# Prompt attention in a hybrid decoder layer: query, key and bias rows laid out by head, and a third half-step scored inside the projection

## The chip, the core and the metric

The kernel runs on one core of a Trainium2 chip. A core has a matrix engine (PE, whose weight loads are listed apart as PEld), a vector engine (DVE), an activation engine (ACT), a general engine (POOL) and a queue engine (SP) that here only issues transfers; each works through its own list of instructions in order, and they wait for each other by semaphores. Transfers (DMA) move data between DRAM, the on-chip memory (SBUF) and back; matrix products end in PSUM banks. The metric is the device time of one execution in microseconds (us), the median over several runs.

## The reference

One layer of a decoder is computed for a prompt of 2048 tokens and for a group of 8 samples of 4 tokens, both in float32. The projection `z = h @ w_in` is cut into the inputs of four branches; the prompt's stick-breaking attention is the branch that the change touches:

```python
h = rms_norm(x, pre_g)
z = h @ w_in
ca, cb, cg, pu, pg, q, k, v, sg, mq, mg = jnp.split(z, ...)   # conv, pool, attention, memory

def sb_block(q, k, v, bias, q_pos, k_pos):
    z = einsum('nqhd,nkhd->nhqk', q, k) * (SB_HEAD_DIM ** -0.5) + bias[None, :, None, None]
    mask = (k_pos[None, :] < q_pos[:, None])[None, None]
    log_beta = log_sigmoid(z)
    log_1m = where(mask, log_sigmoid(-z), 0.0)
    rc = cumsum(log_1m, axis=3, reverse=True)
    a = exp(where(mask, log_beta + rc - log_1m, -inf))
    return einsum('nhqk,nkhd->nqhd', a, v)
```

There are 8 heads of 64 and one bias per head. So the weight of a key is beta = sigmoid(z) times the product of (1 - beta) over all keys between it and the query: a running product along the keys, from the query backwards. The outputs of all branches are multiplied by gates, joined, multiplied by `w_out`, normalised and added to the input.

## The kernel before, in words

The work runs in three long stages. After a short start the **projection** goes through the columns of `w_in` in groups, for the first 1056 columns of tokens (half 0) and then the other 1024 (half 1); each product is three passes over high and low parts of the operands (line 251). `z_evac` takes each finished tile out of PSUM. Beside it run side generators (`tasks`): the depthwise convolution on DVE (`conv_dw`, line 642, 12 tile steps of `cacc` at the end of the last channel), the memory attention and the sample group's paged attention. The **prompt attention** then goes over 4 pairs of heads (`hp`) and 4 blocks of 512 queries (`qb`), and for each over the key blocks `kc` from the diagonal downwards. A piece of 2 times 128 queries of one head is a half-step, named `hp_qb_kc_hh_q2` (hh: head of the pair; q2: 0 or 2, its first block of 128 queries). The **out-projection** comes last.

For one half-step `sb_scores` multiplies queries with keys into a PSUM tile `S` (two products of 128 and of 66 rows: high parts, low parts, and two rows that add the bias), `sb_gates` makes beta in `be` and 1 - beta in `gam` on ACT, DVE runs the product along the keys (`tensor_tensor_scan`, tile `E`; its second operand `ZM` is a PSUM tile copied by ACT from `zm`, which POOL fills), POOL multiplies `be` by `E`, PE transposes the result (`turn`, line 1398), ACT copies it out, and PE multiplies it with the values (line 1410). Where `rest_of` holds, 1 - beta is made on DVE (line 1358) instead of ACT.

Queries and keys reach this stage through DRAM: `z_evac` (line 721) writes a tile's high and low part with one transfer into `qd` or `kd`, whose layout has the two heads of a pair as 128 partitions; `bias_rows` writes the bias and rows of ones into `bd` (line 467); `load` (lines 1260 to 1281) reads 16 transfers per (hp, qb): for each head the key's high part twice, the query's high and low part, the key's low part, the query's high part again, and the two bias rows of each.

The first two half-steps, 0_0_0_0_0 and 0_0_0_1_0, are scored early: `sb_early` runs as a side generator at the end of the projection, starts once the sample group is done, and keeps 1 - beta and beta of both in the tile `early`.

The order of every engine but PE is set when the program is built, by a scheduler that simulates the program; PE runs in the order in which the code is written. Transfers are issued in order on SP's list, too. The convolution's second part (`conv_post`, lines 1460 to 1500) loads `cy` from DRAM (line 1471) and adds four channel groups on POOL into `cs` (line 1478); its first load and sum are side work with no place in the written order of POOL and SP.

Of the kernel before, what the change touches and what calls it, by code (L numbers as in the profile page):

```python
# [8 lines left out]
F32 = mybir.dt.float32  # L9
# [3 lines left out]
AF = mybir.ActivationFunctionType  # L13
# [5 lines left out]
P = 128  # L19
D = 1024  # L20
ND = D // P
SEQ = 2048
# [70 lines left out]
def kernel(  # L93
# [29 lines left out]
    dram = ctx.enter_context(tc.tile_pool(name="dram", bufs=1, space=DRAM))  # L123
    qd = dram.tile([4, P, 2, SEQ], F32, name="qd")
    kd = dram.tile([4, P, 2, SEQ], F32, name="kd")
    vd = dram.tile([SEQ, 512], F32, name="vd")
# [17 lines left out]
    mvd = dram.tile([4, P, 2, 2 * P], F32, name="mvd")  # L144
    bd = dram.tile([NH + 1, 2, 512], F32, name="bd")
    c11d = dram.tile([8, P, 512], F32, name="c11d")
# [307 lines left out]
    def bias_rows():  # L454

        b = zc.tile([NH, 1], F32, name="brow")
        sp.dma_start(b, sb_bias.rearrange("o h -> h o"))
        hl = zc.tile([NH, 2], F32R, name="bhl")
        t = k4("brows", [P, 2, 512], F32)
        pool.memset(t[: NH + 1], 1.0)  # L460
        for _ in range(3):
            yield
        dve.tensor_copy(hl[:, 0:1], b)
        dve.tensor_tensor(out=hl[:, 1:2], in0=b, in1=hl[:, 0:1].bitcast(F32), op=ALU.subtract)
        for x in range(2):
            dve.tensor_copy(t[:NH, x], hl[:, x : x + 1].bitcast(F32).to_broadcast([NH, 512]))
        sp.dma_start(bd, t[: NH + 1])

# [237 lines left out]
    def z_evac(part, kind, c, ti, c0, c1, ps, s):  # L706
# [5 lines left out]
        if kind in ("q", "k"):  # L712
            zt = small(f"zt{nm}")
            before = table[6] if nm == "0q0_0" else casts[-1] if state["mem"] else None
            with tc.issue_after(before.ins) if before is not None else ExitStack():
# [4 lines left out]
                               op=ALU.subtract)  # L720
            wq.dma_start((qd if kind == "q" else kd)[c, :, :, tok : tok + np_], hl[:, :, :np_].bitcast(F32))
            if N > np_:
# [533 lines left out]
    def sb_loader(sbr):  # L1256
# [3 lines left out]
        def load(hp, qb):  # L1260
            tok = slice(512 * qb, 512 * qb + 512)
            Q = []
            for hh in range(2):
                pr = slice(64 * hh, 64 * hh + 64)
                slot = qb if qb or hp % 2 == 0 else 4
                kts = [(sbr if slot < 2 else KT["pool"]).tile([P, 512], F32R, tag=f"k{n}{slot}", name=f"k{n}{hp}_{qb}_{hh}",
                                                              bufs=2) for n in "hl"]
                qt_ = sbr.tile([P, 2, 512], F32R, tag="Q", name=f"Q{hp}_{qb}_{hh}", bufs=4)
                for x in range(2):
                    hx = slice(64 * x, 64 * x + 64)  # L1270
                    sp.dma_start(kts[0][hx].bitcast(F32), kd[hp, pr, 0, tok])
                    sp.dma_start(qt_[hx, 0].bitcast(F32), qd[hp, pr, x, tok])
                sp.dma_start(kts[1][:64].bitcast(F32), kd[hp, pr, 1, tok])
                sp.dma_start(qt_[:64, 1].bitcast(F32), qd[hp, pr, 0, tok])
                sp.dma_start(kts[1][64:66].bitcast(F32), bd[2 * hp + hh])
                sp.dma_start(qt_[64:66, 1].bitcast(F32), bd[NH])
# [12 lines left out]
    def sb_scores(S, q2, w, Q, kts):  # L1289
        for j in range(2):  # L1290
            c = slice(P * (q2 + j), P * (q2 + j + 1))
            pe.matmul(S[:, j, :w], lhsT=Q[:, 0, c], rhs=kts[0][:, :w], start=True, stop=False)  # L1292
            pe.matmul(S[:, j, :w], lhsT=Q[:66, 1, c], rhs=kts[1][:66, :w], start=False, stop=True)  # L1293

# [5 lines left out]
    def sb_early(load, values, blk, sbr, bps, early):  # L1300

        room = sbr.tile([P, 16, P], F32, tag="V", name="early", bufs=2).rearrange("p (n j b) c -> p n j (b c)", n=4, j=2)
        for n in range(2):
            blk[0, n] = load(0, n)
        values(0)
        for _ in range(4):
            yield
        for hh in range(2):
            S = bps.tile([P, 512], F32, tag="AT", name=f"Se{hh}", bufs=2).rearrange("p (j k) -> p j k", j=2)
            Q, KT, _ = blk[0, 0]  # L1310
            sb_scores(S, 0, 2 * P, Q[hh], KT[0, hh, 0])
            early[hh] = room[:, 2 * hh], room[:, 2 * hh + 1]
            sb_gates(S, 2 * P, *early[hh])
            yield

    def sb_prompt(load, loaded, sb, bps, ops, zmp, early, values_of, flags, newest):
# [18 lines left out]
        def score(hp, qb, kc, hh, q2, Q, KT, carry):  # L1335
# [4 lines left out]
            w = ns[1]  # L1340
            rest_of = q2 == 2 and (dg or hh == 0)
            if (hp, qb, q2) == (0, 0, 0):
                ga, be = early[hh]
            else:
                S = ops.tile([P, 2, 512], F32, tag="S", name=f"S{nm}", bufs=2)
                sb_scores(S, q2, w, Q[hh], KT[hp, hh, kc])
                be = sb.tile([P, 2, 512], F32, tag="be", name=f"be{nm}", bufs=BEB)
                g_ = gam[count["pair"] % 3]
                count["pair"] += 1
                ga = g_[:, :, 512 - w : 512]  # L1350
                sb_gates(S, w, None if rest_of else ga, be[:, :, :w])
# [853 lines left out]
```

## Time and profile before

| | us |
|---|---|
| median of the runs (3 runs) | 2327.63 |
| lowest and highest run | 2325.99, 2337.69 |
| the profiled execution's own time | 2329.11 |
| its span in the profile | 2327.4 |
| projection, about | 30 to 1474 of the span |
| prompt attention, about | 1474 to 1880 |
| out-projection, to the end | 1880 to 2327 |
| busy PE / DVE / ACT / POOL | 2252.0 / 1716.6 / 1079.3 / 1317.9 |

A row of a timeline gives the start in us from the start of the span, the busy time in us, the engine, the line, the operation and its tiles (written<-read, buffer numbers left out), the shape and a count; in brackets stands the idle time of that engine just before and what ended it. SPq rows are transfers being issued. A row of a view by stretches of time gives the stretch and its length, then the busy us and (in brackets) the instructions of PE, PEld, DVE, ACT and POOL, the granted share of PE's clock, the mean busy share of the DMA engines and GB/s. A row of waits tells which instruction waited for which: us in total, times, longest.

### The profile page before, as it was taken

What the parts mean: (1) busy time and instruction counts of PE and PEld (TensorE: products, weight loads), DVE (VectorE), ACT (ScalarE), POOL (GpSimd) and SP (SyncE); (2) the same over time, 40 slices, a digit from 0 to 9 for tenths busy, and PEclk for the clock granted to TensorE, in tenths of its full rate; (3) what the DMA queues carried; (4) which work ended last, traced back from release to release, by engine and by line L of the source; (5) the groups of instructions that cost most, each with busy time, mean ns of one, the idle gap of its engine ahead of it and who ended that gap; (6) DMA issues with size and microseconds to landing.
All of it is one profiled execution on the core that took longest, in us unless ns stands there. A gap on an engine that the chain in (4) does not pass through costs nothing. (4 is left out here: it accounts for less than half of the span.)

```text
span 2327.4 us, 43469 instructions
## 1 busy us (share of the span) xinstructions
PE 2252.0 (97%) x16512; PEld 1815.3 (78%) x16512; DVE 1716.6 (74%) x2303; ACT 1079.3 (46%) x1975; POOL 1317.9 (57%) x1410
## 2 busy tenths in 40 slices
PE   7999999999999999999999999999999999999997
PEld 7998888888888777777777777667766668787775
DVE  5343786969647764477786867899999876686997
ACT  5332343342442322224242334588888876453553
POOL 3554546556474655545546455489999964432332
PEclk9999999999999999999999999899999999999999
DMA  6689977878679899987977884666545207876774
GB/s 213 200 284 323 337 265 261 285 249 286 245 254 307 308 355 335 336 287 270 319 253 233 298 275 149 166 199 200 158 132 133 76 20 233 290 231 190 248 248 145
DMA packets 338189, 558.32 MB, mean 240 GB/s; under 512 B 29163, under 2 KB 213611, under 8 KB 321581
## 3 DMA queue, kind: packets, MB, share of 16 engines
q1 hardware_dynamic: 282604, 286.83, 39.8%
q0 software_dynamic: 55376, 268.72, 32.4%
q8 instruction: 130, 2.13, 0.4%
q14 instruction: 79, 0.64, 0.1%
HBM read 465.35 MB, written 90.72 MB: 239 GB/s over the span
## 5 line engine op out<-in xcount | busy, mean ns | idle before, releaser
L990 DVE STREAM_TRANSPOSE T<-kt 128x1024 f32<-128x1024 f32 x256 | 308.6, 1226 | 182.2 <-PE sSA L1003 174.7
L957 POOL DMA_INDIRECT vt<-in_cache_v_dram,idv x256 | 253.1, 989 | 257.0 <-PE sO L1042 195.9
L642 DVE SCALAR_TENSOR_TENSOR cacc<-U,par,cacc 128x512 f32<-128x512 f32 x480 | 359.8, 750 | 11.0
L1379 POOL TENSOR_TENSOR be<-be,E 128x512 f32<-128x512 f32 (+4 forms) x316 | 314.1, 1004 | 25.4 <-DVE E L1370 13.0
L957 POOL DMA_INDIRECT kt<-in_cache_k_dram,idk x128 | 128.7, 1006 | 196.1 <-DVE T L990 155.2
L1370 DVE TENSOR_TENSOR_SCAN E<-gam,cr,ZM 128x513 f32<-128x513 f32 x192 | 230.7, 1261 | 4.7 <-POOL csq L1490 1.0
L2024 PE MATMUL acc<-wohi,mh 128*128 128x512 f32 (+1 forms) x480 | 192.0, 400 | 0.2 <-ACT mh L1748 0.2
L2024 PE MATMUL acc<-wolo,mh 128*128 128x512 f32 (+1 forms) x480 | 188.4, 392 | 0.7 <-DVE wolo L1659 0.7
L2024 PE MATMUL acc<-wohi,ml 128*128 128x512 f32 x448 | 177.2, 395 | 6.5 <-DVE ml L1759 6.5
L1400 ACT COPY at<-AT 128x512 f32<-128x512 f32 (+1 forms) x288 | 154.6, 598 | 44.2 <-PE AT L1398 39.0
L1398 PE MATMUL AT<-ident,be 128*128 128x128 f32 x1082 | 155.9, 283 | 17.4 <-ACT at L1400 11.7
L1398 PEld LDWEIGHTS AT<-ident,be 128*128 128x128 f32 x1082 | 122.1, 144 | 59.6 <-issue 23.8
L1298 ACT ACTIVATE be<-S 128x1024 f32<-128x1024 f32 (+1 forms) x158 | 154.2, 976 | 9.9 <-PE S L1293 7.5
L1003 PE MATMUL sSA<-T,W 128*32 128x128 f32 x4096 | 138.2, 276 | 1.8 <-DVE T L990 1.4
L1410 PE MATMUL av<-at,V 128*64 128x256 f32 (+1 forms) x1152 | 137.0, 378 | 0.5 <-DVE sgt L1414 0.3
L1292 PE MATMUL S<-kh,Q 128*128 128x512 f32 (+1 forms) x316 | 134.6, 430 | 1.5 <-ACT be L1298 1.5
L1003 PEld LDWEIGHTS sSA<-T,W 128*32 128x32 f32 x4096 | 104.5, 109 | 36.7 <-issue 29.1
L1759 DVE TENSOR_TENSOR ml<-mr,mh 128x512 fp32r<-128x512 f32 x108 | 92.3, 862 | 40.4 <-ACT mh L1748 39.6
L1410 PEld LDWEIGHTS av<-at,V 128*64 128x64 f32 x1152 | 76.4, 138 | 58.4 <-issue 23.5
L1042 PE MATMUL sO<-vt,saT 128*32 128x512 f32 x1024 | 122.0, 592 | 0.0
L1293 PE MATMUL S<-kl,Q 66*128 66x512 f32 (+1 forms) x316 | 120.7, 386 | 0.0
L1748 ACT CAST mh<-mr 128x512 fp32r<-128x512 f32 (+1 forms) x120 | 70.3, 594 | 89.9 <-PE acc L2024 26.0
(591 smaller groups left out, 6254.5 us busy)
## 6 DMA issues: line engine op xcount, KB each, us to landing
mr<-mixd SPq DMA_DIRECT2D x32, 512.0 KB
Q<-qd SPq DMA_DIRECT2D x96, 128.0 KB
mr<-mixd SPq DMA_DIRECT2D x48, 256.0 KB
xtp<-in_x_prompt_dram SPq DMA_DIRECT2D x16, 512.0 KB
kh<-kd SPq DMA_DIRECT2D x64, 128.0 KB
ws<-in_w_out_dram SPq DMA_DIRECT2D x16, 512.0 KB
wsd<-ws SPq DMA_DIRECT2D x16, 512.0 KB
msd<-mr SPq DMA_DIRECT2D x32, 256.0 KB
```

The lines of the kernel that those rows point to most:

```text
L642: dve.scalar_tensor_tensor(out=ps, in0=U[:, a + k : a + k + H], scalar=wd[:, k : k + 1], in1=ps, op0=ALU.mult, op1=ALU.add)
L957: pool.indirect_dma_start(out=dst, out_offset=None, in_=rows, in_offset=bass.IndirectOffsetOnAxis(ap=idx, axis=0))
L990: S["turn"] = dve.transpose(T[:, 2 * hh : 2 * hh + 2].rearrange("p s j t -> p (s j t)"), kt[:, 2 * hh : 2 * hh + 2].rearrange("p s j d -> ...
L1003: pe.matmul(sSs[n][32 * g : 32 * g + 32, P * ml : P * (ml + 1)], lhsT=W[:, jj, :], rhs=T[:, :, jj, :], start=i == 0, stop=i == 3, tile_pos ...
L1292: pe.matmul(S[:, j, :w], lhsT=Q[:, 0, c], rhs=kts[0][:, :w], start=True, stop=False)
L1298: act.activation(out=be, in_=S[:, :, :w], func=AF.Sigmoid)
L1370: dve.tensor_tensor_scan(out=E[:, j][:, ::-1], data0=g_[:, j][:, ::-1], data1=ZM[:, 0:1].to_broadcast([P, 513]), initial=carry[hh, q2][:, ...
L1379: newest.append(pool.tensor_tensor(out=be[:, j, :m], in0=be[:, j, :m], in1=E[:, j, 513 - w : 513 - w + m], op=ALU.mult).ins)
L1398: pe.transpose(ap_[:, n : n + P], A[hp, qb, kc, hh, qt][:, P * r : P * (r + 1)], ident)
L1400: act.copy(at[:, :n], ap_[:, :n])
L1410: pe.matmul(av[64 * hh : 64 * hh + 64, c], lhsT=V[:, 4 * kc + r, 64 * hh : 64 * hh + 64], rhs=ats.pop((hp, qb, kc, hh, q2, r)), start=dg a ...
L2024: pe.matmul(o[:rows], lhsT=m[a][:, k, :rows], rhs=W[prod, 4 * h + k][w], start=not cont and h == k == n == 0, stop=h == 1 and k == 3 and n ...
```

## The change

1. **Layout.** `qd` and `kd` become `[4, 2, 130, 2048]`: each head has 2 rows for bias or ones, 64 rows and 64 rows. For queries these are the high and the low part, for keys the low and the high part. `bd` is gone; `bias_rows` writes the bias rows into `kd` and ones into `qd` with 8 transfers of a block of 512 tokens each instead of one transfer, from two tiles (`brows`, `bones`).
2. **Stores.** `z_evac` writes the high and the low part of a query or key tile with two transfers in place of one; there are 40 such tiles.
3. **Loads.** `load` issues 10 transfers per (hp, qb) in place of 16: the query's two parts come as one transfer of 128 rows, and the low key part and the second query operand come with their bias rows as 66 rows.
4. **Early scores.** `sb_early` waits for two steps of its generator instead of four and scores three half-steps: 0_0_0_0_0, 0_0_0_1_0 and 0_0_0_0_2. The third uses two PSUM tiles, one with the tag of the values' accumulator (`av`) and one with that of the transposes (`AT`). ACT makes only beta of these; 1 - beta is made on DVE in `rest`, since `rest_of` now holds for all three.

```diff
-    qd = dram.tile([4, P, 2, SEQ], F32, name="qd")
-    kd = dram.tile([4, P, 2, SEQ], F32, name="kd")
+    qd = dram.tile([4, 2, P + 2, SEQ], F32, name="qd")
+    kd = dram.tile([4, 2, P + 2, SEQ], F32, name="kd")
...
-    bd = dram.tile([NH + 1, 2, 512], F32, name="bd")
...
-        sp.dma_start(bd, t[: NH + 1])
+        for qb in range(4):
+            for dst, src in ((kd, t), (qd, one)):
+                sp.dma_start(dst.rearrange("a b r t -> (a b) r t")[:, 0:2, 512 * qb : 512 * qb + 512], src[:NH])
+            yield
...
-            wq.dma_start((qd if kind == "q" else kd)[c, :, :, tok : tok + np_], hl[:, :, :np_].bitcast(F32))
+            for x in range(2):
+                r = 2 + DH * (x if kind == "q" else 1 - x)
+                wq.dma_start((qd if kind == "q" else kd)[c, :, r : r + DH, tok : tok + np_], hl[:, x, :np_].bitcast(F32))
...
                 for x in range(2):
-                    hx = slice(64 * x, 64 * x + 64)
-                    sp.dma_start(kts[0][hx].bitcast(F32), kd[hp, pr, 0, tok])
-                    sp.dma_start(qt_[hx, 0].bitcast(F32), qd[hp, pr, x, tok])
-                sp.dma_start(kts[1][:64].bitcast(F32), kd[hp, pr, 1, tok])
-                sp.dma_start(qt_[:64, 1].bitcast(F32), qd[hp, pr, 0, tok])
-                sp.dma_start(kts[1][64:66].bitcast(F32), bd[2 * hp + hh])
-                sp.dma_start(qt_[64:66, 1].bitcast(F32), bd[NH])
+                    sp.dma_start(kts[0][64 * x : 64 * x + 64].bitcast(F32), kd[hp, hh, 66:130, tok])
+                sp.dma_start(qt_[:, 0].bitcast(F32), qd[hp, hh, 2:130, tok])
+                sp.dma_start(kts[1][:66].bitcast(F32), kd[hp, hh, 0:66, tok])
+                sp.dma_start(qt_[:66, 1].bitcast(F32), qd[hp, hh, 0:66, tok])
...
-        for _ in range(4):
-            yield
-        for hh in range(2):
-            S = bps.tile([P, 512], F32, tag="AT", name=f"Se{hh}", bufs=2).rearrange("p (j k) -> p j k", j=2)
-            Q, KT, _ = blk[0, 0]
-            sb_scores(S, 0, 2 * P, Q[hh], KT[0, hh, 0])
-            early[hh] = room[:, 2 * hh], room[:, 2 * hh + 1]
-            sb_gates(S, 2 * P, *early[hh])
+        Q, KT, _ = blk[0, 0]
+        for _ in range(2):
+            yield
+        o = 0
+        for hh, q2, tags in ((0, 0, ("AT",)), (1, 0, ("AT",)), (0, 2, ("av", "AT"))):
+            w = P * (q2 + 2)
+            be = early[hh, q2] = room[:, o : o + 2 * w].rearrange("p (j k) -> p j k", j=2)
+            o += 2 * w
+            S = [bps.tile([P, 512], F32, tag=t, name=f"Se{hh}{q2}{t}", bufs=2 if t == "AT" else 1) for t in tags]
+            if len(S) == 1:
+                S = S[0].rearrange("p (j k) -> p j k", j=2)
+                sb_scores([S[:, j] for j in range(2)], q2, w, Q[hh], KT[0, hh, 0])
+                act.activation(out=be, in_=S, func=AF.Sigmoid)
+            else:
+                sb_scores(S, q2, w, Q[hh], KT[0, hh, 0])
+                for j in range(2):
+                    act.activation(out=be[:, j], in_=S[j], func=AF.Sigmoid)
             yield
...
-            rest_of = q2 == 2 and (dg or hh == 0)
-            if (hp, qb, q2) == (0, 0, 0):
-                ga, be = early[hh]
+            ahead = (hp, qb) == (0, 0) and (hh, q2) in early
+            rest_of = ahead or q2 == 2 and (dg or hh == 0)
+            g_ = gam[count["pair"] % 3]
+            count["pair"] += 1
+            ga = g_[:, :, 512 - w : 512]
+            if ahead:
+                be = early[hh, q2]
```

The scheduler places the work of the other engines anew, and at three places around the end of the projection the lists differ. The last numbers of the names are buffer numbers, and the pair's number in front is left off; `early` is the tile of the early betas, `cs` the convolution's sum over channel groups, `sg1cg_1` and `sg1sg_1` the last two gate tiles of the projection.

On POOL, at the end of the projection, before the change the list reads:

```order
L1106 AFFINE_SELECT nM<-nM 32x32
L1362 MEMSET early 128x2 x2
L1322 MEMSET zm 128x384
L1323 COPY zm<-ident 128x128
L1329 MEMSET gam_14901 128x2
L1329 MEMSET gam_14903 128x2
L1329 MEMSET gam_14905 128x2
L1362 MEMSET be_0_0_0_2_14914 128x2
L1379 TENSOR_TENSOR early<-early,E_0_0_0_0_14916 128x127
```

and with the change:

```order
L1110 AFFINE_SELECT nM<-nM 32x32
L1488 TENSOR_TENSOR cs_19906<-cy_19566 128x256
L1488 TENSOR_TENSOR cs_19906<-cs_19906,cy_19566 128x256 x2
L1331 MEMSET zm 128x384
L1332 COPY zm<-ident 128x128
L1338 MEMSET gam_14942 128x2
L1338 MEMSET gam_14944 128x2
L1338 MEMSET gam_14946 128x2
L1372 MEMSET early 128x2 x3
L1389 TENSOR_TENSOR early<-early,E_0_0_0_0_14950 128x127
```

The three sums into `cs`, which stood some 60 rows further down, behind POOL's products for query block 2, key block 0, head 1 (`be_2_0_1_0`), now stand ahead of `zm`.

On SP, the queue of transfers, the rows around the first load of `cy` read before:

```order
L1271 DMA kh_0_1_15678<-kd 64x512 x2
L1431 DMA sgt_2_15254<-gsd 128x512
L1273 DMA kl_0_1_15679<-kd 64x512
L1275 DMA kl_0_1_15679<-bd 2x512
L1285 DMA V_15689<-vd 128x16x128
L1471 DMA cy_19614<-ydw 128x4x256
```

and with the change:

```order
L1285 DMA V_14783<-vd 128x16x128
L748 DMA gsd<-sg1sg_0_14797 128x512
L651 DMA ydw<-acc_3_1_14919 128x512
L748 DMA gcd<-sg1cg_1_14843 128x512
L566 DMA mixd<-mo_3_512_14856 128x4x128
L1274 DMA Q_2_0_14973<-qd 128x512
L1276 DMA Q_2_0_14973<-qd 66x512
L1095 DMA vsn<-vsd 32x512
L1481 DMA cy_19566<-ydw 128x4x256
L748 DMA gsd<-sg1sg_1_14900 128x512
```

The load of `cy` moved from behind the loads of later blocks to a place among the projection's last stores. With the change it waits for the last product of `z1sg_1`, since its buffer lies where the projection's operands lie.

On ACT, at the end of the projection, before:

```order
L575 CAST pT_3_512_14547<-mpt_3_512_256_14768 128x2x256
L732 ACTIVATE sg1cg_1_14802<-z1cg_1_14775 128x512
L648 COPY acc_3_1_14878<-cacc_3_1_14584 128x512
L732 ACTIVATE sg1sg_1_14852<-z1sg_1_14818 128x512
L1297 ACTIVATE early<-Se_14833 128x512
L1298 ACTIVATE early<-Se_14833 128x512
L1297 ACTIVATE early<-Se_14858 128x512
L1298 ACTIVATE early<-Se_14858 128x512
L1298 ACTIVATE be_0_0_0_2_14914<-S_0_0_0_2_14909 128x1024
L1325 COPY ZM<-zm 128x512
```

and with the change:

```order
L577 CAST pT_3_512_14594<-mpt_3_512_256_14803 128x2x256
L650 COPY acc_3_1_14919<-cacc_3_1_14631 128x512
L1318 ACTIVATE early<-Se00AT 128x512
L736 ACTIVATE sg1cg_1_14843<-z1cg_1_14810 128x512
L1318 ACTIVATE early<-Se10AT 128x512
L1322 ACTIVATE early<-Se02av 128x512
L1322 ACTIVATE early<-Se02AT 128x512
L736 ACTIVATE sg1sg_1_14900<-z1sg_1_14865 128x512
L1298 ACTIVATE be_0_0_1_2_14962<-S_0_0_1_2_14957 128x1024
L1334 COPY ZM<-zm 128x512
```

The copy of the convolution's last accumulator now stands ahead of the gates and the early betas, and on DVE the 12 steps that it waits for stand in one run ahead of the gates; PE has the first early scores after 12 of the 24 products of `z1cg_1`, the second behind the memory attention's product, and the third (`Se02av`, `Se02AT`) after 12 of the 24 products of `z1sg_1`. `Se02av` uses the PSUM bank that this copy frees.

More of the change, by code (lines that the diff above doesn't have):

```diff
@@ L458, in bias_rows @@
         hl = zc.tile([NH, 2], F32R, name="bhl")
-        t = k4("brows", [P, 2, 512], F32)
-        pool.memset(t[: NH + 1], 1.0)
+        t, one = k4("brows", [P, 2, 512], F32), k4("bones", [P, 2, 512], F32)
+        pool.memset(one[:NH], 1.0)
         for _ in range(3):
@@ L1263, in load @@
             for hh in range(2):
-                pr = slice(64 * hh, 64 * hh + 64)
                 slot = qb if qb or hp % 2 == 0 else 4
@@ L1291, in sb_scores @@
             c = slice(P * (q2 + j), P * (q2 + j + 1))
-            pe.matmul(S[:, j, :w], lhsT=Q[:, 0, c], rhs=kts[0][:, :w], start=True, stop=False)
-            pe.matmul(S[:, j, :w], lhsT=Q[:66, 1, c], rhs=kts[1][:66, :w], start=False, stop=True)
+            pe.matmul(S[j][:, :w], lhsT=Q[:, 0, c], rhs=kts[0][:, :w], start=True, stop=False)
+            pe.matmul(S[j][:, :w], lhsT=Q[:66, 1, c], rhs=kts[1][:66, :w], start=False, stop=True)
     def sb_gates(S, w, ga, be):
@@ L1300, in sb_early @@
     def sb_early(load, values, blk, sbr, bps, early):
-        room = sbr.tile([P, 16, P], F32, tag="V", name="early", bufs=2).rearrange("p (n j b) c -> p n j (b c)", n=4, j=2)
+        room = sbr.tile([P, 16, P], F32, tag="V", name="early", bufs=2).rearrange("p b c -> p (b c)")
         for n in range(2):
@@ L1340, in score @@
             w = ns[1]
-            rest_of = q2 == 2 and (dg or hh == 0)
-            if (hp, qb, q2) == (0, 0, 0):
-                ga, be = early[hh]
+            ahead = (hp, qb) == (0, 0) and (hh, q2) in early
[5 more added lines that the diff above has]
+                be = early[hh, q2]
             else:
                 S = ops.tile([P, 2, 512], F32, tag="S", name=f"S{nm}", bufs=2)
-                sb_scores(S, q2, w, Q[hh], KT[hp, hh, kc])
+                sb_scores([S[:, j] for j in range(2)], q2, w, Q[hh], KT[hp, hh, kc])
                 be = sb.tile([P, 2, 512], F32, tag="be", name=f"be{nm}", bufs=BEB)
-                g_ = gam[count["pair"] % 3]
-                count["pair"] += 1
-                ga = g_[:, :, 512 - w : 512]
                 sb_gates(S, w, None if rest_of else ga, be[:, :, :w])
```

## The prediction

> **What bounds the kernel now.** I read the page first, then the span by stretches: the three stages, and the turn from the first to the second on a finer grid.
>
> ```profile
> span 2327.4 us, 43469 instructions
> PE 2252.0 (97%) x16512; PEld 1815.3 (78%) x16512; DVE 1716.6 (74%) x2303; ACT 1079.3 (46%) x1975; POOL 1317.9 (57%) x1410
> ```
>
> ```profile
> 30.00:1474.00 1444.00, 1431.39 (x11691) 1182.53 (x11689) 976.54 (x1359) 486.27 (x911) 768.01 (x710) 1.00 0.81 276
> 1500.00:1880.00 380.00, 364.66 (x2555) 266.49 (x2554) 356.61 (x360) 323.30 (x501) 353.31 (x474) 0.98 0.51 142
> 1880.00:2327.00 447.00, 415.67 (x2052) 333.98 (x2050) 342.19 (x528) 230.58 (x495) 168.57 (x154) 0.98 0.64 208
> ...
> 1474.00:1476.31 2.31, 0.83 (x6) 0.59 (x4) 0.61 (x2) 2.31 (x5) 0.80 (x6) 1.00 0.50 134
> 1476.31:1490.30 13.99, 11.17 (x43) 7.84 (x42) 12.82 (x18) 6.86 (x12) 10.56 (x22) 0.51 1.04 283
> ```
>
> PE is busy for 1431 of 1444 us in the projection. In the attention PE (365 of 380), DVE (357) and POOL (353) are all nearly full and pass each half-step on: none has room to catch up, so a late start of that stage moves its end by as much. The out-projection is PE's again. The one loose place is the turn at 1474 to 1490, where PE stands still and then runs at half clock (0.51). PE's waits from 1470 to 1880 are for ACT, DVE and POOL, and none for a transfer; of seven groups these are the largest and the one that the early scores touch:
>
> ```profile
> PE AT L1398 <- ACT at L1400: 11.7, 12, 3.0
> ...
> PE S L1292 <- ACT be L1298: 1.5, 1, 1.5
> ```
>
> **Layout, stores and loads: nothing.** The page has the loads that are merged:
>
> ```profile
> Q<-qd SPq DMA_DIRECT2D x96, 128.0 KB
> ...
> kh<-kd SPq DMA_DIRECT2D x64, 128.0 KB
> ```
>
> Sixteen (hp, qb) of 16 issues become 10: 96 issues fewer. No instruction of PE waits for one of these in the rows above, and the work that hides them is the previous block's. Were that cover gone, each would cost its issue time, about 0.5 us on SP. The projection gains 40 stores and 7 bias transfers on SP. The queue stands there with room: the load of a weight tile at 245.82, first used by its cast at 267.68, is 21.9 us early.
>
> ```profile
> 245.82 0.38 SPq L233 DMA_DIRECT2D wr0pg<-in_w_in_dram  x1
> L241 ACT CAST whi0pg<-wr0pg x1: 1052/1052/1052, 267.7 to 267.7; 128x1024 fp32r<-128x1024 f32 x1
> ```
>
> Forty-seven issues of that row's 0.38 (18 us over a stage of 1444) do not use that up. I take 0 for both; the bounds are -1.9 us (the DVE's two waits for transfers in the attention, 1.3 and 0.6, gone) and +3.0 us (all eight bias transfers at 0.38 in front of a tile that is waited for).
>
> ```profile
> DVE nrb L1139 <- DMA ngc<-gnd: 1.3, 1, 1.3
> ...
> DVE sgt L1414 <- DMA sgt<-gsd: 0.6, 1, 0.6
> ```
>
> **Early scores: what starts the attention.** Its first scan on DVE now starts at 1476.31. These rows lead to it:
>
> ```profile
> 1474.84 0.42 POOL L1322 MEMSET zm<- 128x384 f32 x1
> 1475.20 0.30 POOL L1323 COPY zm<-ident 128x128 f32<-128x128 f32 x1
> ```
> ```profile
> 1471.70 0.59 ACT L648 COPY acc<-cacc 128x512 f32<-128x512 f32 x1 [6.63 <-DVE cacc L642]
> ...
> 1472.67 0.60 ACT L1297 ACTIVATE early<-Se 128x512 f32<-128x512 f32 x1
> ...
> 1475.53 0.63 ACT L1325 COPY ZM<-zm 128x512 f32<-128x512 f32 x1
> ```
> ```profile
> 1460.41 3.91 DVE L642 SCALAR_TENSOR_TENSOR cacc<-U,par,cacc 128x512 f32<-128x512 f32 x5
> ...
> 1466.97 4.70 DVE L642 SCALAR_TENSOR_TENSOR cacc<-U,par,cacc 128x512 f32<-128x512 f32 x6
> ...
> 1476.31 1.88 DVE L1367 TENSOR_TENSOR_SCAN E<-early,ZM 128x128 f32<-128x128 f32 x4
> ...
> 1485.70 1.06 DVE L1358 TENSOR_SCALAR gam<-be 128x1024 f32<-128x1024 f32 x1 [0.90 <-ACT be L1298]
> ```
>
> POOL fills `zm`, ACT copies it to `ZM`, and 0.15 us after that copy the scan starts. In the changed lists POOL has the three sums into `cs` ahead of `zm`. POOL works in order, so `zm` now waits for the load of `cy`, and that for the last product of `z1sg_1`. What is queued behind the waiting sum is all that POOL has to do for the attention; ACT's copy to `ZM` waits for it, DVE for that, and PE's transposes for POOL's first products. I follow it step by step.
>
> PE first. It reached the early scores in the middle of `z1sg` at 1468.45:
>
> ```profile
> 1468.45 0.28 PE L1292 MATMUL Se<-kh,Q 128*128 128x256 f32 x1
> ...
> 1468.93 0.40 PE L251 MATMUL z1sg<-xhi,whi1sg 128*128 128x512 f32 x1
> ...
> 1471.71 0.28 PE L1292 MATMUL Se<-kh,Q 128*128 128x256 f32 x1
> ```
>
> One set of four takes 1468.93 - 1468.45 = 0.48, and the 12 products behind it 2.78. With two sets ahead PE stands at `Se02av` at 1468.45 + 0.96 = 1469.41. This tile wants the bank from ACT's copy of the accumulator, and that wants the 12 steps of `cacc`: 1460.41 + 12 x 0.783 (4.70 / 6) = 1469.81, and the copy of 0.59 ends at 1470.40. `Se02av` takes 0.48 (1470.88), `Se02AT` waits for ACT's first early beta (0.60 behind the copy: 1471.00) and ends at 1471.48. The 12 products end at 1474.26 in place of 1471.71, and a tail of some 0.3 for the last one gives 1474.6.
>
> Then the load. On SP only `gcd`, `mixd`, two `Q` and `vsn` stand near it, and these can go while PE finishes. With one such issue still in hand (0.38 to 0.6 us in SP's rows), `cy` goes out at about 1475.2. Of four later loads of `cy` in the same trace three were waited for on POOL:
>
> ```profile
> 1992.72 0.45 SPq L1471 DMA_DIRECT2D cy<-ydw  x1
> ...
> 2020.06 1.52 SPq L1471 DMA_DIRECT2D cy<-ydw  x1
> ...
> 2042.15 0.37 SPq L1471 DMA_DIRECT2D cy<-ydw  x1
> ...
> 2071.60 0.38 SPq L1471 DMA_DIRECT2D cy<-ydw  x1
> ```
> ```profile
> 2000.08 0.74 POOL L1478 TENSOR_TENSOR cs<-cy 128x256 f32<-128x256 f32 x1 [0.89 <-DMA cy<-ydw]
> ...
> 2025.67 0.74 POOL L1478 TENSOR_TENSOR cs<-cy 128x256 f32<-128x256 f32 x1 [3.16 <-DMA cy<-ydw]
> ...
> 2046.03 0.74 POOL L1478 TENSOR_TENSOR cs<-cy 128x256 f32<-128x256 f32 x1
> ...
> 2077.78 0.81 POOL L1478 TENSOR_TENSOR cs<-cy 128x288 f32<-128x288 f32 x1 [2.28 <-DMA cy<-ydw]
> ```
>
> From issue to use the three took 7.36, 5.61 and 6.18 us; the one from 2042.15 was in time with 3.88, so the bounds are 3.9 and 7.4. I take the middle one that was waited for, 6.18: `cy` is there at 1481.4. [...]
>
> Then POOL: the sums, from their rows further down now,
>
> ```profile
> 1534.88 0.73 POOL L1478 TENSOR_TENSOR cs<-cy 128x256 f32<-128x256 f32 x1
> 1535.69 1.87 POOL L1478 TENSOR_TENSOR cs<-cs,cy 128x256 f32<-128x256 f32 x2
> ```
>
> take 2.68 to 1537.56, so they end at 1484.1; `zm` takes 0.66 (1474.84 to 1475.50), ACT's copy 0.66 with its hand-over, and 0.15 later the scan starts: 1485.5 against 1476.31, **+9.2 us** (6.9 to 10.4 with the bounds of the landing). What the early scores save comes to nothing behind this: ACT's 4 passes of about 0.6 for `gam`, PE's 1.5 us of waiting for a bank, and the four products of 0_0_0_0_2 before the turn. DVE's three added passes for 1 - beta fit into the idle time before 1485.
>
> **What comes back.** The three sums no longer stand at 1534.88, in the full part of the attention, where DVE idles right behind them:
>
> ```profile
> 1535.33 0.84 DVE L1358 TENSOR_SCALAR gam<-be 128x1024 f32<-128x1024 f32 x1 [1.58 <-ACT be L1298]
> ...
> 1546.01 0.70 DVE L1358 TENSOR_SCALAR gam<-be 128x1024 f32<-128x1024 f32 x1 [2.63 <-ACT be L1298]
> ```
>
> I take -2.6, since POOL is as full as DVE there and its list shortens by 2.68; the bounds are 0 (the idle time has other causes) and -2.7. The half clock after the start costs DVE only the 0.90 of idle time quoted at 1485.70, so a shorter or longer one moves little while PE's work is hidden behind the scans: 0, at best -0.9.
>
> Sum: 9.2 - 2.6 = **+6.6 us** (+3.3 to +10.4) on an execution of 2329.1, whose span is 1.7 shorter. That execution lies 1.5 above the median of the runs, so +6.6 on 2327.6 gives **2334 us**. A difference under 0.5% (11.6 us) can't be told from no change in this kernel, so this counts as the same.
>
> **The rivals.**
> (1) *The load is early enough.* If `z1sg` ends no later than before and `cy` lands in under 3.9 us, the sums stand in POOL's idle time (1.5 of 2.31 us idle at 1474) and what is left is the gain: -2.6 for the sums, -0.9 for the half clock: 2324. For it: POOL idles here. Against: in the rows POOL's idle time ends at 1474.8, before `cy` can even be issued. 0.12.
> (2) *The merged loads count.* 1.9 us of DVE's waits go and the start is as late as forecast: +4.7, 2332. The DMA share in the attention is 0.51, so not likely: 0.05.
> (3) *Slower than the bound.* PE now stands idle from about 1475.5 to 1486 and starts cold. Before, the half clock held for 13.99 us though PE was busy for 11.17 of them. From the late start on, each us at half clock in which PE is the bound costs half a us. With +6.6, another 5.0 us are wanted, so 10 us more of half clock with PE as the bound, to about 1510; or the landing of 7.4 with no recovery (+10.4) and 1.2 more, a late load of the first keys. That would be 2339 to 2343. For it: PE is at 365 of 380 right behind. Against: only 0.90 of DVE's idle time was seen in such a stretch. 0.14.
> (4) *The clock comes back at once.* [...] By rows that is at best the 0.90 that DVE waited: +5.7, 2333. [...] 0.07.
>
> **How the numbers follow.** The forecast has 0.62, its own range 2330 to 2339; with the rivals the chances add to 1. Eight times in 10 lie between 2322 and 2341: the lower end takes in rival 1 and a run 2 us under the median, the upper end the near half of rival 3. Faster by over 0.5% (under 2316) would need two gains that I have no row for: 0.04. Slower by over 0.5% (above 2339.3) is rival 3 with a little of the forecast's upper end: 0.15. The rest, 0.81, is within 0.5%.
>
> **What would show it.** POOL's first sum into `cs` waits for `cy<-ydw` at about 1476 to 1481, `zm` follows at 1484, and the first scan starts at 1485 (within 2 us). `Se02av` waits some 1.0 us for ACT's copy, and the last product of `z1sg` ends near 1474.5. At 1535 no sum stands between POOL's products, and the waits of PE and DVE there shrink. The number of transfers falls by 96 in the attention without any wait of PE going. I am wrong if the first scan starts before 1479, if the time between it and the last product changes by more than 4 us, or if the projection ends elsewhere than 2 to 3 us later.

## The result and the profile after: 11% slower, in the projection

The changed kernel takes 2596.9 us (median of 6 runs, 2594.1 to 2599.5) against 2335.7 for the kernel before (6 runs): the ratio is 1.1127, with a 95% interval of 1.1105 to 1.1149. The forecast was 2334, with eight chances in ten between 2322 and 2341. The page of the changed kernel begins so:

```profile
span 2597.3 us, 43448 instructions
PE 2295.5 (88%) x16512; PEld 1846.2 (71%) x16512; DVE 1715.7 (66%) x2305; ACT 1078.1 (42%) x1974; POOL 1313.7 (51%) x1410
```

The engines do the same work (DVE, ACT and POOL within 5 us of before, PE 43 us more). The span is 270 us longer, and PE's idle time in it grows from 75.4 to 301.8 us. The span cut into stretches shows where. Before, the stretches at the start read:

```profile
30.00:200.00 170.00, 166.00 (x1267) 157.93 (x1266) 69.00 (x128) 58.81 (x117) 84.25 (x75) 0.99 0.74 241
200.00:300.00 100.00, 100.00 (x900) 89.29 (x900) 62.96 (x81) 31.43 (x65) 54.21 (x50) 1.00 0.91 325
```

and with the change (the last three are the second half's key, value and query columns):

```profile
30.00:200.00 170.00, 124.42 (x773) 118.94 (x771) 51.17 (x108) 40.54 (x78) 61.18 (x56) 0.87 0.44 146
200.00:300.00 100.00, 60.42 (x502) 53.97 (x503) 16.87 (x20) 19.34 (x40) 21.90 (x19) 0.77 0.52 168
...
900.00:1000.00 100.00, 62.95 (x415) 46.65 (x415) 23.81 (x28) 15.10 (x28) 31.14 (x25) 0.80 0.49 167
1000.00:1100.00 100.00, 74.65 (x580) 55.15 (x579) 46.90 (x60) 18.89 (x34) 38.31 (x40) 0.86 0.79 262
1100.00:1200.00 100.00, 48.87 (x342) 34.22 (x341) 17.16 (x21) 11.39 (x21) 27.47 (x24) 0.73 0.46 160
```

Nearly all of the loss lies in these two places, and they are the places where queries and keys are projected and stored. The transfers are *less* busy there than before (0.44 against 0.74 of the DMA engines), so it is no lack of bandwidth as a whole. PE's longest waits in the projection (us in total, times, longest):

```profile
PE nt1v L378 <- ACT zt1v L732: 37.5, 3, 25.4
PE sSA L1007 <- ACT saT L1036: 34.4, 2, 34.0
PE smt L1203 <- DMA mkb<-in_cache_mem_k_dram: 32.6, 3, 15.8
PE nt0k L378 <- ACT zt0k L718: 32.0, 4, 18.5
PE nt1k L378 <- ACT zt1k L718: 24.9, 2, 12.4
```

ACT is not the cause; between 30 and 320 us it waits itself, for stores that have not landed and so have not freed their tiles:

```profile
ACT nat0k L385 <- DMA out_dram<-nat0k: 26.7, 4, 15.0
ACT zt0k L718 <- DMA out_dram<-nat0k: 22.2, 3, 12.2
```

The transfer named there is an old one that the change didn't touch. It stands in SP's queue behind the new ones, and even its issue takes longer. These are its issues before and then with the change (shortest, median and longest in ns, then the first and the last start in us):

```profile
L389 SPq DMA_DIRECT2D out_dram<-nat0k x12: 372/562/1385, 106.1 to 168.7; - x12
```
```profile
L388 SPq DMA_DIRECT2D out_dram<-nat0k x12: 383/2642/4563, 145.0 to 264.5; - x12
```

What the new stores do shows best in a moment when all else stands still. These are two stretches of the changed kernel in which no instruction runs on any engine, while key stores are on their way (the last two columns are the mean share of the 16 DMA engines and GB/s):

```profile
1018.00:1020.00 2.00, 0.00 (x0) 0.00 (x0) 0.00 (x0) 0.00 (x0) 0.00 (x0) 0.50 0.13 51
1020.00:1022.60 2.60, 0.00 (x0) 0.00 (x0) 0.00 (x0) 0.00 (x0) 0.00 (x0) 0.50 0.12 44
```

0.125 is 2 of 16: here the kernel waits for transfers that two DMA engines move, at some 50 GB/s. (Idle stretches in which other transfers are under way too show a higher share, 0.56 from 1022.60 to 1028.00.) The changed store has the outer dimension "head of the pair", of size 2, and then 64 rows; the store before had 128 rows with two parts each. From 38.51 to 51.52 us of the kernel before SP issues nothing but three such query stores; these are its row and two half microseconds in which two of them move:

```profile
38.51 13.01 SPq L721 DMA_DIRECT2D qd<-hl0q  x3
```
```profile
40.00:40.50 0.50, 0.50 (x7) 0.33 (x5) 0.35 (x1) 0.50 (x2) 0.07 (x1) 1.00 0.99 369
...
43.00:43.50 0.50, 0.50 (x6) 0.50 (x5) 0.47 (x2) 0.50 (x1) 0.00 (x0) 1.00 1.02 378
```

So the old store was moved at a share of 0.99 to 1.02, all 16 engines, and 369 to 378 GB/s; the changed one at 0.12 to 0.13 and 44 to 51 GB/s. That the outermost dimension makes the difference is not shown by these rows; the runs with two and with four blocks below test it.

The rate gives the size, once the other transfers are counted. These are the query and key stores of the first half, before (12 and 12) and with the change (24 and 24), and then those of the second half with the change:

```profile
L721 SPq DMA_DIRECT2D qd<-hl0q x12: 513/526/650, 26.8 to 98.2; - x12
L721 SPq DMA_DIRECT2D kd<-hl0k x12: 519/520/1914, 104.0 to 168.1; - x12
```
```profile
L725 SPq DMA_DIRECT2D qd<-hl0q x24: 485/539/2732, 25.8 to 133.5; - x24
L725 SPq DMA_DIRECT2D kd<-hl0k x24: 491/672/6785, 141.3 to 263.9; - x24
...
L725 SPq DMA_DIRECT2D kd<-hl1k x16: 497/2666/9852, 872.5 to 1023.2; - x16
...
L725 SPq DMA_DIRECT2D qd<-hl1q x16: 477/2113/12510, 1073.8 to 1191.0; - x16
```

A tile of 128 rows and 384 tokens is 393 kB in its two parts, which by an estimate takes 8.0 us if the rate is 49 GB/s, within the 44 to 51 of the rows above; one of 256 tokens takes 5.4. Sixteen of the first and eight of the second would keep two engines busy for 171 us, in a stretch that took 141 us before and takes 238 now. In the second half, 16 tiles of 512 tokens want 10.7 us each, again 171 us.

But 171 us don't fill 238. What is missing is the other traffic. These rows cover the time from the first to the last of these stores in each half, before and then with the change:

```profile
26.80:168.10 141.30, 137.30 (x973) 133.10 (x971) 61.61 (x120) 50.74 (x98) 72.83 (x66) 0.99 0.68 221
...
774.60:956.00 181.40, 180.39 (x1411) 134.84 (x1411) 100.42 (x123) 50.11 (x90) 104.33 (x95) 1.00 0.97 341
```
```profile
25.80:263.90 238.10, 161.84 (x1060) 153.77 (x1058) 64.75 (x126) 54.30 (x105) 76.99 (x69) 0.84 0.42 138
...
872.50:1191.00 318.50, 204.32 (x1497) 150.56 (x1499) 104.01 (x128) 52.71 (x96) 108.19 (x102) 0.81 0.60 203
```

An estimate from them: the other transfers of the first half's stretch (138 GB/s over 238.1 us, less the 8.4 MB of the stores) are 24.5 MB. Spread evenly over 16 engines at 24.5 GB/s each, they take 62 us of every engine. With the 171 us of stores that makes 234 of the 238.1 us on the two engines. In the second half the others are 56 MB or 144 us, and 171 + 144 = 315 of 318.5. So these two engines would be nearly full in both halves, while the mean share of all 16 is only 0.42 and 0.60. No view shows single engines, so this is argued from the sums and not shown.

The forecast's own place, the turn to the attention, did in the main what was foretold, only 255 us later. The last gate before the change (`sg1sg`), and then rows of SP, POOL and DVE in the changed kernel:

```profile
1472.82 0.69 DVE L742 TENSOR_TENSOR sg1sg<-z1sg,sg1sg 128x512 f32<-128x512 f32 x1 [1.15 <-ACT sg1sg L732]
```
```profile
1729.04 0.38 SPq L1481 DMA_DIRECT2D cy<-ydw  x1
```
```profile
1734.51 0.72 POOL L1488 TENSOR_TENSOR cs<-cy 128x256 f32<-128x256 f32 x1 [32.82 <-DMA cy<-ydw]
1735.31 1.52 POOL L1488 TENSOR_TENSOR cs<-cs,cy 128x256 f32<-128x256 f32 x2
1736.77 0.42 POOL L1331 MEMSET zm<- 128x384 f32 x1
```
```profile
1727.86 0.69 DVE L746 TENSOR_TENSOR sg1sg<-z1sg,sg1sg 128x512 f32<-128x512 f32 x1 [5.39 <-ACT sg1sg L736]
...
1738.08 3.84 DVE L1377 TENSOR_TENSOR_SCAN E<-gam,ZM 128x128 f32<-128x128 f32 x6 [8.19 <-ACT ZM L1334]
```

The sum waits for `cy`, `zm` for the sum, `ZM` for `zm` and the first scan for `ZM`: 10.2 us behind the projection's last gate (`sg1sg`), where it was 3.5 before (1472.82 to 1476.31).

One step didn't come. `Se02av` follows the product before it without a gap, so PE doesn't wait for its bank:

```profile
1723.03 0.40 PE L250 MATMUL z1sg<-xhi,wlo1sg 128*128 128x512 f32 x1
1723.26 0.39 PE L1292 MATMUL Se02av<-kh,Q 128*128 128x512 f32 x1
...
1726.74 0.40 PE L250 MATMUL z1sg<-xhi,wlo1sg 128*128 128x512 f32 x1
```

So the 269.9 us of longer span split into 255.0 up to the last gate (1727.86 against 1472.82), 6.7 from there to the first scan, and 8.1 in what follows.

### The profile page after: what moved, and what is told of

Same layout as the page of the kernel before. It is cut to its first block, busy times and chain, and to the rows that moved or that the text cites. A ratio compares the mean times of both kernels' runs of the same rounds, so it can differ in the third digit from the quotient of the medians.

```text
span 2597.3 us, 43448 instructions
## 1 busy us (share of the span) xinstructions
PE 2295.5 (88%) x16512; PEld 1846.2 (71%) x16512; DVE 1715.7 (66%) x2305; ACT 1078.1 (42%) x1974; POOL 1313.7 (51%) x1410
## 5 line engine op out<-in xcount | busy, mean ns | idle before, releaser
L1007 PE MATMUL sSA<-T,W 128*32 128x128 f32 x4096 | 143.9, 280 | 36.6 <-ACT saT L1036 34.4
```

The source lines that it names most:

```text
L1007: pe.matmul(sSs[n][32 * g : 32 * g + 32, P * ml : P * (ml + 1)], lhsT=W[:, jj, :], rhs=T[:, :, jj, :], start=i == 0, stop=i == 3, tile_pos ...
```

## The experiments

Three causes were set against each other for the loss in the projection: A, the two DMA engines; B, the number of issues and the order in which SP's transfers wait for each other; C, the layout with 130 rows per head.

**Stores by head.** The changed kernel with each store cut again, so that its outer dimension is 64 rows:

```diff
             for x in range(2):
                 r = 2 + DH * (x if kind == "q" else 1 - x)
-                wq.dma_start((qd if kind == "q" else kd)[c, :, r : r + DH, tok : tok + np_], hl[:, x, :np_].bitcast(F32))
+                for hh in range(2):
+                    wq.dma_start((qd if kind == "q" else kd)[c, hh, r : r + DH, tok : tok + np_],
+                                 hl[64 * hh : 64 * hh + 64, x, :np_].bitcast(F32))
```

> Each store of the change (one part of one tile, both heads: two blocks of 64 rows) is cut again by head: 160 stores of 64 rows in place of 80 of two times 64; all else as in the change. Theory A (a store whose outer dimension has 2 entries is moved by 2 of the 16 DMA engines: the trace of the changed kernel shows a DMA share of 0.12 to 0.13, two sixteenths, from 1018 to 1022.6 with every engine idle): the loss in the projection goes, the time is 2335 to 2345. Theory B (the added issues and the order in which SP's transfers wait for each other cost the time, 262 us for 40 issues): 80 more issues add twice that, about 3100. Theory C (writes into the layout with 130 rows per head are slow, however they are cut): 2590 to 2605.

Measured: 2365.4 us, 1.0133 of before (1.0103 to 1.0163). Twice as many issues as in the change take 232 us away, so B falls as the main cause, and C with it. It ends 20 us above the range of A: these 160 stores still cost something, and the turn costs more than was foretold (both below).

**The old layout with split stores.** The kernel before, each store made as two of 128 rows:

```diff
-            wq.dma_start((qd if kind == "q" else kd)[c, :, :, tok : tok + np_], hl[:, :, :np_].bitcast(F32))
+            for x in range(2):
+                wq.dma_start((qd if kind == "q" else kd)[c, :, x, tok : tok + np_], hl[:, x, :np_].bitcast(F32))
```

> The kernel before with one edit: each store of a query or key tile is made as two, of the high and of the low part, each of 128 rows (80 stores in place of 40), in the old layout. Theory A (two DMA engines): 128 rows use all 16, so no change, 2330 to 2345. Theory B (the number of issues): the whole loss, about 2597. Theory C (the layout): no change.

Measured: 2341.1 us, 1.0041 of before (1.0021 to 1.0061). The same 40 added issues as in the change cost some 10 us, not 262. The last gate of its profile comes at 1479.46, 6.6 later than before:

```profile
1479.46 0.69 DVE L743 TENSOR_TENSOR sg1sg<-z1sg,sg1sg 128x512 f32<-128x512 f32 x1 [1.15 <-ACT sg1sg L733]
```

**Two blocks alone.** The kernel before, with no more than a spare row behind each head in DRAM. As many stores, issues and loads as before; only the outer dimension of a store is now 2 (the indices of the loads follow the layout):

```diff
-    qd = dram.tile([4, P, 2, SEQ], F32, name="qd")
-    kd = dram.tile([4, P, 2, SEQ], F32, name="kd")
+    qd = dram.tile([4, 2, DH + 1, 2, SEQ], F32, name="qd")
+    kd = dram.tile([4, 2, DH + 1, 2, SEQ], F32, name="kd")
...
-            wq.dma_start((qd if kind == "q" else kd)[c, :, :, tok : tok + np_], hl[:, :, :np_].bitcast(F32))
+            wq.dma_start((qd if kind == "q" else kd)[c, :, :DH, :, tok : tok + np_], hl[:, :, :np_].bitcast(F32))
```

> The kernel before with one edit: the DRAM tiles of queries and keys get an unused 65th row per head, so that each of the 40 stores, still one per tile and with both parts, has an outer dimension of 2 blocks. Loads and issues as before. Theory A (two DMA engines): the same bytes go through two engines as in the change, so about the same loss, 2500 to 2650. Theory B (the number of issues): no change, 2330 to 2345. Theory C (the layout with 130 rows and its bias rows): no change or a part of the loss.

Measured: 2564.0 us in one run. An unused row brings back nearly all of the loss. Its last gate, and two stretches in which all engines stand still:

```profile
1711.63 0.69 DVE L742 TENSOR_TENSOR sg1sg<-z1sg,sg1sg 128x512 f32<-128x512 f32 x1 [1.15 <-ACT sg1sg L732]
```
```profile
201.00:203.00 2.00, 0.00 (x0) 0.00 (x0) 0.00 (x0) 0.00 (x0) 0.00 (x0) 0.50 0.13 49
...
209.00:211.00 2.00, 0.00 (x0) 0.00 (x0) 0.00 (x0) 0.00 (x0) 0.00 (x0) 0.50 0.14 47
```

The gate is 238.8 us later than before (change: 255.0), at the same 0.13 of the DMA engines.

**Four blocks.** The same with a spare row behind each 32 rows; the loads then read pieces of 32 rows:

```diff
+    qd = dram.tile([4, 4, 33, 2, SEQ], F32, name="qd")
+    kd = dram.tile([4, 4, 33, 2, SEQ], F32, name="kd")
...
+            wq.dma_start((qd if kind == "q" else kd)[c, :, :32, :, tok : tok + np_], hl[:, :, :np_].bitcast(F32))
```

> The kernel before with an unused 33rd row behind each 32 rows of queries and keys in DRAM, so that each of the 40 stores has an outer dimension of 4 blocks; the loads read pieces of 32 rows (28 in place of 16 per pair and block). Theory A (the engines used go by that dimension): four engines in place of two, each store takes half as long, and the projection loses less than half of the 238 us that two blocks cost: its last gate comes 30 to 110 us later than before. If any gap between the heads' rows costs the same: 230 to 250 later. If only two blocks are bad: no loss.

Measured: 2456.6 us in one run.

```profile
1572.25 0.69 DVE L742 TENSOR_TENSOR sg1sg<-z1sg,sg1sg 128x512 f32<-128x512 f32 x1 [1.15 <-DMA Q<-qd]
```
```profile
49.00:51.00 2.00, 2.00 (x12) 1.98 (x12) 0.13 (x1) 0.00 (x0) 0.00 (x0) 0.62 0.27 95
...
171.00:173.00 2.00, 0.00 (x0) 0.00 (x0) 0.00 (x0) 0.00 (x0) 0.00 (x0) 0.50 0.27 102
```

The gate is 99.4 us later than before, and in these two stretches, in the first of which PE still runs, the share is 0.27, some four engines of 16, at 95 and 102 GB/s, twice the 47 and 49 of two blocks. So the stores with 2, 4 and 128 in the outer dimension were moved at shares of 0.13, 0.27 and 0.99 to 1.02, and from two blocks to four the loss falls by more than half. (28 us more are lost behind the first scan; the added pieces of the loads, 12 per pair and block, are the only edit there.) The sum with the other traffic, made in the same way, gives 222 of the 227.0 us between the first and the last store of the second half here, and for two blocks alone 233 of 233.1 and 310 of 305.8. In the first half of this kernel it gives only 146 of 180.7 us, so there full engines don't account for the time.

**Half and half.** The changed kernel, by head in the projection's first half, in two blocks in its second:

```diff
-                wq.dma_start((qd if kind == "q" else kd)[c, :, r : r + DH, tok : tok + np_], hl[:, x, :np_].bitcast(F32))
+                for hh in (slice(0, 1), slice(1, 2)) if part == 0 else (slice(0, 2),):
+                    wq.dma_start((qd if kind == "q" else kd)[c, hh, r : r + DH, tok : tok + np_],
+                                 hl[64 * hh.start : 64 * hh.stop, x, :np_].bitcast(F32))
```

> The changed kernel, with the stores by head (64 rows each) in the projection's first half (24 of 40 tiles) and the two-block stores of the change in its second half (16 tiles). Theory A (two DMA engines, held up the more where the sample group's gathers use the same engines): in the change's trace the first store of half 1 is 100 us later than before and the last one 235 us, so half 1 keeps a loss of 120 to 150 and half 0 loses its own: 2485 to 2525. If the loss went by the number of tiles (16 of 40): 2365 + 0.4 x 232 = about 2458. If only the start of the kernel is open to it: about 2365.

Measured: 2518.2 us in one run, inside the range of A. Its last gate:

```profile
1640.42 0.69 DVE L748 TENSOR_TENSOR sg1sg<-z1sg,sg1sg 128x512 f32<-128x512 f32 x1 [2.49 <-ACT sg1sg L738]
```

Against the run with all stores by head (1493.25) the 16 tiles of the second half cost 147 us, 9.2 each; the 24 of the first half cost the rest of the change's loss, 1727.86 - 1640.42 = 87, or 3.6 each. The second half loses more per tile. Its tiles are larger (512 tokens against 341 on average), the sample group's gathers run beside it, and the DMA engines had less room there before (a share of 0.97 against 0.68 in the rows above). How much each of these does was not separated.

**Layout and merged loads without the early scores.** Stores by head, and `sb_early` and the head of `score` as in the kernel before:

```diff
-        for _ in range(2):
+        for _ in range(4):
             yield
-        for hh, q2, tags in ((0, 0, ("AT",)), (1, 0, ("AT",)), (0, 2, ("av", "AT"))):
+        for hh in range(2):
...
-            rest_of = ahead or q2 == 2 and (dg or hh == 0)
+            rest_of = q2 == 2 and (dg or hh == 0)
```

> The stores by head of the first run of this study, and early scoring as in the kernel before (two half-steps, both gates on ACT): layout, bias rows and merged loads alone. Theory A with the forecast's step (the convolution's sum is placed ahead of the tile zm only where the third half-step is scored early): 2328 to 2337, and 6 to 9 us less than the run with the stores by head and the early scores. If the early scores cost nothing: the same as that run within 3 us. Theory B: about 3100.

Measured: 2347.9 us, 1.0071 of before (1.0047 to 1.0096). Last gate and first scan of this run, and of the run with stores by head and early scores:

```profile
1491.13 0.69 DVE L748 TENSOR_TENSOR sg1sg<-z1sg,sg1sg 128x512 f32<-128x512 f32 x1 [2.13 <-DMA Q<-qd]
...
1494.68 1.89 DVE L1369 TENSOR_TENSOR_SCAN E<-early,ZM 128x128 f32<-128x128 f32 x4 [0.80 <-ACT ZM L1327]
```
```profile
1493.25 0.69 DVE L748 TENSOR_TENSOR sg1sg<-z1sg,sg1sg 128x512 f32<-128x512 f32 x1 [5.05 <-ACT sg1sg L738]
...
1505.43 1.00 DVE L1379 TENSOR_TENSOR_SCAN E<-gam,ZM 128x128 f32<-128x128 f32 x2 [10.14 <-ACT ZM L1336]
```

Two things follow. With 96 issues fewer in the attention this run needs 2346.1 - 1494.7 = 851.4 us from the first scan to the end of its span, and the kernel before 2327.4 - 1476.3 = 851.1: by these two executions the merged loads bring nothing. (DVE's waits for `sgt<-gsd`, part of the gain that the prediction held possible, even grow from 0.6 to 5.2 us.) And with stores alike the early scores cost 17 us (2365.4 - 2347.9), 10.8 of them up to the first scan. The range foretold (to 2337) was missed because the last gate comes 18.3 us later than before. The 120 added stores are the largest edit there; what the layout and the bias rows do was not separated from them.

Theory D was that the early scores cost time only through the convolution's sum ahead of `zm`; theory E, that they cost it by themselves.

**Early scores alone.** The kernel before with the change's `sb_early` and `score`, and nothing else of it; the sum then stays far down POOL's list. The edit is the last part of the change's diff.

> The kernel before with the change's early scores alone (three half-steps, beta alone on ACT, start after two steps): old layout, stores and loads. In its lists the convolution's sum stays behind the first blocks' products and does not stand ahead of zm. Theory D (the early scores cost time only through that sum ahead of zm): no loss, 2324 to 2334, and the first scan within 2 us of where it is before. Theory E (scoring three half-steps within the projection costs time by itself, by PE's wait for the bank and DVE's passes for 1 - beta): 2340 to 2350, as between the runs with stores by head with and without the early scores (17 us).

Measured: 2325.7 us against 2329.2, a ratio of 0.9991 (0.9975 to 1.0007): no difference. E falls, in the old layout. (The profiled execution of this kernel was its slowest, 2337.8, so of its trace only the distance within it is used.)

```profile
1478.35 0.69 DVE L742 TENSOR_TENSOR sg1sg<-z1sg,sg1sg 128x512 f32<-128x512 f32 x1 [3.48 <-ACT sg1sg L732]
1480.31 3.82 DVE L1377 TENSOR_TENSOR_SCAN E<-gam,ZM 128x128 f32<-128x128 f32 x6
```

The first scan starts 2.0 us behind the last gate in place of 3.5, so the early scores do save 1.5 us at this place; the whole doesn't show it.

**The sum late.** Stores by head and early scores, and POOL's first sum held back:

```diff
-                for c in range(3):
-                    pool.tensor_tensor(out=sums[i], ...)
+                with tc.issue_after(newest[41]) if i == 0 else ExitStack():
+                    for c in range(3):
+                        pool.tensor_tensor(out=sums[i], ...)
```

> The kernel with stores by head and early scores (2365), with one edit: the convolution's first sum may be issued only behind POOL's 42nd product of the attention, about where it stands in the kernel before. Theory D: the first scan comes 7 to 9 us earlier after the projection's last gate (3.5 us after it in place of 12.2), and the time is 2350 to 2359. Theory E: 2362 to 2368.

Measured: 2352.0 us, 1.0096 of before (1.0068 to 1.0123), 13.4 less than with the sum ahead (11.8 if each is taken against the kernel before that was run beside it, 2352.0 - 2329.2 and 2365.4 - 2330.8).

```profile
1494.50 0.69 DVE L748 TENSOR_TENSOR sg1sg<-z1sg,sg1sg 128x512 f32<-128x512 f32 x1 [2.65 <-ACT sg1sg L738]
1496.47 3.82 DVE L1379 TENSOR_TENSOR_SCAN E<-gam,ZM 128x128 f32<-128x128 f32 x6
```

The scan follows the gate by 2.0 us in place of 12.2. D holds in the main. Against the run without early scores (2347.9 - 2330.8 = 17.1) a rest of 22.8 - 17.1 = 5.7 us is left, and the intervals of these two kernels overlap. No version of this study beats the kernel before; the early scores in the old layout equal it.

## Why the prediction was wrong, step by step

- **"Layout, stores and loads: nothing."** This is the step that failed, in its half on the stores: taken as 0, with +3.0 as the upper bound; the change's loss up to the last gate is 255 us. I priced a store by what its issue takes on SP (0.38 us) and by the room in that queue. I did not ask how long it takes to land and how many DMA engines carry it, though the diff changes just that: `[c, :, :, ...]` over 128 rows became `[c, :, r : r + DH, ...]`, two blocks of 64. The kernel with a spare row shows that this alone costs 239 us. The room of 21.9 us that I measured for a weight tile was true, but by the estimate above a store keeps two engines busy for 2.7 to 5.4 us, and a few tiles use that room up. The issue itself took longer, too, up to 12.5 us for one store of the second half. No rival held this either, and the range left out even the bounds that were named for this term (-1.9 and +3.0).
- **The added issues themselves.** Taken as 0. With 128 rows outermost 40 more cost 6.6 us up to the last gate, and with 64 rows 120 more (without the early scores) 18.3: some 0.15 to 0.17 us each, from one execution of each kernel. By the medians the whole kernels lose 10.3 and 17.1 us. Small, but not hidden.
- **The merged loads: 0.** Right as far as one execution of each tells: 851.4 against 851.1 us from the first scan on.
- **The first scan: +9.2 us.** Right in the mechanism, the load that holds up the sum, `zm` and the scan, and near in size, in part by luck. With stores alike the scan is 10.8 later with the early scores than without them, just above the bound of 10.4, and holding the sum back takes 10.2 of its distance from the last gate away. Three terms are off in the changed kernel and nearly cancel: `cy` is issued 1.9 us behind the end of the last product of `z1sg` (0.6 was foretold), takes 5.47 from issue to use (6.18), and the sums take 2.26 to the start of `zm` (2.68). The wait of PE at `Se02av` (1.0) didn't come. POOL did wait for `cy`, so the rival of an early load falls. With stores by head the gate is 2.1 later with the early scores than without them (2.55 was foretold for the last products); what makes that up is open.
- **What comes back: -2.6 us.** Wrong. From the first scan to the start of the last one it takes 429.7 us with the sum early and 429.7 with the sum late, so nothing comes back:

```profile
L1382 DVE TENSOR_TENSOR_SCAN E<-gam,cr,ZM x192: 1244/1257/1282, 1520.0 to 1935.1; 128x513 f32<-128x513 f32 x192
```
```profile
L1382 DVE TENSOR_TENSOR_SCAN E<-gam,cr,ZM x192: 1244/1257/1283, 1511.0 to 1926.2; 128x513 f32<-128x513 f32 x192
```

To the end of the span the run with the sum early needs 2367.1 - 1505.4 = 861.7, with the sum late 2356.8 - 1496.5 = 860.3, and without early scores 851.4. These first two executions lie 3.5 and 6.6 us above the medians of their kernels, so a part of the 9 to 10 us is chance. What makes up the rest stays open; with early scores alone the whole time did not change.

- **The rival "slower than the bound"** named the half clock. The granted clock does fall in the changed kernel (0.73 to 0.87 on average in the five stretches above), but in the projection, and PE stands still for 25 to 51% of the time in these stretches: the mean over the whole run is 0.944 with the change, 0.984 with stores by head and 0.990 before. Behind the first scan, where this rival and the one on the clock's return had it, the clock is 0.63 for 9.92 us and then 1.00, in place of 0.51 for 13.99 us; no gain in time shows from that.

## What to carry to other kernels

A layout that makes loads contiguous can break the stores: write down the access pattern of each transfer on both sides and look at the outermost dimension, since 2 there meant a share of 0.12 to 0.14, two of 16 DMA engines, and 44 to 51 GB/s, where 128 had given 0.99 to 1.02 and 369 to 378 GB/s, and a single spare row per head was enough to cause it. Price a store by its landing, not by its issue, and ask for how long per tile its engines are kept busy: by the estimate above 7.1 us of store stood against 5.9 us of work on average (171 and 141 us for 24 tiles), more than room in a queue can hide, and by the same estimate 62 us of other traffic came on top. Here the waits named innocent transfers behind the stores (ACT waited up to 15.0 us for `out_dram<-nat0k`); stretches in which all engines stood still and the share of the DMA engines was near two sixteenths (0.12 and 0.13) pointed at the guilty ones.

## What the runs showed of the hardware

- The share of DMA engines in stretches in which little but such stores is under way is 0.12 to 0.14 with two blocks and 0.27 with four, at 44 to 51 and 95 to 102 GB/s: some 22 to 26 GB/s for each of two or four engines. With 128 rows outermost it is 0.99 and 1.02, at 369 and 378 GB/s: 23 to 24 for each of 16.
- With the two-block stores ahead of them in SP's queue, unchanged stores were late: ACT waited up to 15.0 us for `out_dram<-nat0k`, and the issue of that store took a median of 2.64 us in place of 0.56.
